# Fourier–Hyena encoder layer: within each sum, the products of the first parts placed ahead of those with a second part, and some casts and copies placed elsewhere

## The chip, the cores and the metric

The kernel runs on one core of one Trainium2 chip. TensorE (PE) multiplies matrices into PSUM, VectorE (DVE), ScalarE (ACT) and GpSimd (POOL) work elementwise, SyncE (SP) and POOL issue the transfers between HBM and SBUF. The metric is the device time of the one launch in microseconds, as a median over runs. Lower is better.

## The reference, cut to what matters

One encoder layer is applied to two sequences of 1024 rows and 1024 columns, called b=0 and b=1, in float32:

```
xn = rmsnorm(x, g_pre);  p = xn @ w_in                     # 1024 x 8192, split into
fv, fg, hv(3x), hg, mg(2x) = split(p)                      # 1024 columns each
y_f = (real(fft2 of fv by groups) * silu(fg)) @ w_fourier_out
v, x1, x2 = split(short_conv(hv))                          # width 3 along the rows
z = v
for n, gate in enumerate((x1, x2)):
    z = gate * long_conv(z, kf[:, n], d[n])                # by FFT of length 2048
y_h = (z * silu(hg)) @ w_hyena_out
g_f, g_h = split(sigmoid(mg + b_merge))
out = x + rmsnorm((g_f * y_f + g_h * y_h) @ w_out, g_post)
```

The filters kf come from a small network of sines and exponentials.

## The kernel before, in words

**Precision.** Almost all matrix products are made of rounded numbers. `split` (L168) turns a float32 tile into two parts that PE takes: the first part `h` is the rounded value, cast on ACT (L171), and the second part `l` is what is left, source minus `h`, a subtraction on DVE or POOL (L181). A product of a weight block w and a data block x is then three matmuls into one PSUM sum: h·h, h·l and l·h. `mm3` (L372) emits these three in a row, for one block of 128 rows of the contraction after the other. In the names below `wh`, `wl` are the two parts of a weight block, `xh`, `xl` those of the data, `bh`, `bl` and `yh`, `yl` those of the long convolution's data.

**Stages, in order of time.** (1) `phase_fourier`: normalisation, a copy of the normalised x to HBM (`d_x`), and the two-dimensional FFT as matrix products. (2) `phase_main`: first the 16 filter spectra (`pft`, `pXf`), with projections of b=0 between them as filling (`spill_gate`, PSUM tile `pin`, 128 by 1024, two banks); then `branches`, the long convolutions: 32 steps, 16 for each b. (3) `phase_gates`: the last projections of b=1 as 2 by 2 block products with fewer multiplications (`times`, PSUM `pg`). (4) `phase_out`: products with w_fourier_out (`pyf`) and w_hyena_out (`pyh`), 32 of each, and beside them the loading and splitting of w_out (`beside`, `blocks`, `sums`). (5) `last_rows`: the product with w_out (`po`, again `times`), the norm and the stores.

**A step of `branches`.** `conv_front` of the next step (transposes `tph`, the radix-4 `butterfly` on DVE, casts `bh`, subtractions `bl`) and `gates` of the next step (projection of x1 or x2) are traced ahead of `conv_back` of the step itself. `conv_back` runs four groups: `pX` (forward matmuls), a product with the spectrum on DVE, `yh` on ACT, `yl` on DVE, `pT` (inverse matmuls). In every second step with b=0, `gates` also multiplies x2 by silu(hg): for channels c below 6 the projection hg lies in HBM already, is loaded into a tile `sg` (tag `gt`, three buffers, shared with other tiles), passes through Silu on ACT (L937) and is multiplied into x2 on POOL.

**Weights.** `inproj` (L726) takes its blocks in two halves q of four blocks each: load `wr`, cast `wh` on ACT, `wl` on POOL (1472 matmuls of each of the three kinds use them). For b=1 the conv projections reload `wh`, `wl` from HBM. In the output stages `weight` (L1116) loads `wr` by POOL's queue, with `wh` on ACT and `wl` on DVE; three sets of buffers take turns.

**What sets the order.** The code is traced, and a scheduler of the tile framework, with a cost model of its own, orders the instructions of each engine ahead of the run. On the chip each engine and each queue takes its instructions in that fixed order, and waits by semaphores. `issue_after(i)` makes what is traced inside it stand behind instruction i on i's engine.

## Time and profile before

| | us |
|---|---|
| median of 3 runs (lowest, highest) | 2466.59 (2461.57, 2469.35) |
| the profiled execution, its own time | 2470.75 |
| its span, from the first to the last instruction | 2469.0 |
| PE busy in the span | 2407.5 (98%) |
| DVE busy | 1912.8 (77%) |
| ACT busy | 1064.4 (43%) |
| POOL busy | 499.0 (20%) |

PE's busy time is the union of matmuls whose modelled ends overlap, so a busy PE can still hold small gaps. An entry "A <- B" in a list of waits means that an instruction of A was idle until B released it; a line such as L194 is that of a helper through which all matmuls go, so groups are told apart by tiles. "PEclk" is the granted share of TensorE's clock.

### The profile page before, as it was taken

The numbers are of one execution on the slowest core, as the hardware profiler recorded it, in microseconds if no ns is written. First come the engines' busy times: TensorE is split into PE (matmuls) and PEld (weight loads), VectorE is DVE, ScalarE is ACT, GpSimd is POOL, SyncE is SP. The second block draws the span as 40 slices with busy tenths as digits, with TensorE's granted clock in tenths as the row PEclk, the third lists the DMA queues.
The fourth block names the chain that finished last, engine by engine and source line by source line (L and its number), as shares of the span: only waits on it lengthen the run. The fifth ranks groups of instructions, "written<-read, shape, count | busy, mean of one in ns | idle before, by whom it ended". The sixth has DMA issues, their size and how long they took to land.

```text
span 2469.0 us, 36969 instructions
## 1 busy us (share of the span) xinstructions
PE 2407.5 (98%) x13196; PEld 2086.9 (85%) x13196; DVE 1912.8 (77%) x3597; ACT 1064.4 (43%) x1919; POOL 499.0 (20%) x516
## 2 busy tenths in 40 slices
PE   6999999999999999999999999999999999999998
PEld 6988888888788888888888888888788788787786
DVE  7687898998649999899889999866556455665677
ACT  5546576766433333333222222323444344444343
POOL 1331213221342443331000000112100111112121
PEclk9999999999999999999999999999999999999999
DMA  7535655555555455545443443435444567775443
GB/s 274 183 122 205 217 182 166 169 180 168 171 174 179 159 176 163 172 149 203 137 134 131 143 142 131 133 128 176 161 162 158 193 218 255 237 268 194 156 160 128
DMA packets 225153, 429.37 MB, mean 174 GB/s; under 512 B 23542, under 2 KB 87255, under 8 KB 224456
## 3 DMA queue, kind: packets, MB, share of 16 engines
q1 hardware_dynamic: 198444, 333.34, 40.7%
q0 software_dynamic: 26336, 93.65, 10.7%
q8 instruction: 104, 1.70, 0.3%
q14 instruction: 81, 0.66, 0.1%
q10 hardware_dynamic: 188, 0.02, 0.0%
HBM read 290.60 MB, written 136.31 MB: 173 GB/s over the span
## 4 chain that ended last, share of the span: by engine, by line
PE 44%; DMA 4%; issue 4%; DVE 1%; POOL 1%; ACT 1%; SPq 0%; DVEq 0%; POOLq 0%; ACTq 0%
PE pin L194 17%; PE pg L194 8%; PE po L194 6%; PE pT L194 4%; PE pyf L194 4%; PE pX L194 4%; PE pyh L194 1%; DMA wr<-in_w_ho 1%; DMA wr<-in_w_fo 1%; POOL wr L1123 1%; PE tph L791 1%; DMA mraw<-d_m 1%; DMA d_m<-yf 1%; DMA t4l<-d_t 0%; DMA d_g<-gt 0%
## 5 line engine op out<-in xcount | busy, mean ns | idle before, releaser
L194 PE MATMUL pin<-xh,wl 128*128 128x512 f32 x1472 | 578.7, 393 | 3.3 <-POOL wl L181 3.3
L194 PE MATMUL pin<-xh,wh 128*128 128x512 f32 x1472 | 578.9, 393 | 1.1 <-DMA wh<-d_w 1.1
L194 PE MATMUL pin<-xl,wh 128*128 128x512 f32 x1472 | 577.5, 393 | 0.6 <-DVE xl L181 0.6
L181 POOL TENSOR_TENSOR wl<-wr,wh 128x512 fp32r<-128x512 f32 x136 | 246.2, 1811 | 1142.8 <-ACT wh L171 739.2
L194 PEld LDWEIGHTS pin<-xh,wl 128*128 128x128 f32 x1472 | 277.8, 189 | 54.9 <-POOL wl L181 4.1
L194 PEld LDWEIGHTS pin<-xl,wh 128*128 128x128 f32 x1472 | 277.7, 189 | 51.8 <-DVE xl L181 1.0
L194 PEld LDWEIGHTS pin<-xh,wh 128*128 128x128 f32 x1472 | 278.0, 189 | 51.3 <-DMA wh<-d_w 1.7
L171 ACT CAST wh<-wr 128x512 fp32r<-128x512 f32 x264 | 162.9, 620 | 326.1 <-PE pin L194 109.4
L194 PE MATMUL pT<-cinv,yh 128*128 128x256 f32 x1024 | 192.4, 283 | 4.4 <-ACT yh L171 4.4
L194 PEld LDWEIGHTS pT<-cinv,yh 128*128 128x128 f32 x1024 | 165.0, 191 | 13.9 <-ACT yh L171 4.9
L171 ACT CAST yh<-y 128x512 fp32r<-128x512 f32 x128 | 79.5, 621 | 202.5 <-DVE y L181 148.0
L181 DVE TENSOR_TENSOR t<-pX,k 128x1024 f32<-128x1024 f32 x128 | 155.5, 1215 | 14.2 <-PE pX L194 13.6
L194 PE MATMUL pyf<-sf,wh 128*128 128x512 f32 x512 | 159.1, 393 | 2.0 <-ACT wh L171 2.0
L194 PE MATMUL pX<-bh,cfwd 128*128 128x256 f32 x768 | 159.7, 286 | 0.0
L194 PE MATMUL pyh<-sh,wh 128*128 128x512 f32 x512 | 158.0, 390 | 1.6 <-ACT wh L171 1.6
L171 ACT CAST bh<-b 128x512 fp32r<-128x512 f32 x144 | 88.9, 619 | 135.1 <-DVE b L181 79.5
L181 DVE TENSOR_TENSOR wl<-wr,wh 128x512 fp32r<-128x512 f32 x128 | 87.4, 686 | 76.7 <-ACT wh L171 76.7
L194 PE MATMUL pT<-cinv,yl 128*128 128x256 f32 x512 | 145.3, 284 | 0.5 <-DVE yl L181 0.5
L194 PEld LDWEIGHTS pX<-bh,cfwd 128*128 128x128 f32 x768 | 125.8, 191 | 3.3
L194 PEld LDWEIGHTS pyf<-sf,wh 128*128 128x128 f32 x512 | 96.7, 189 | 22.8 <-ACT wh L171 2.8
L181 DVE TENSOR_TENSOR bl<-b,bh 128x512 fp32r<-128x512 f32 x144 | 102.6, 721 | 16.6 <-ACT bh L171 16.3
L194 PEld LDWEIGHTS pyh<-sh,wh 128*128 128x128 f32 x512 | 96.0, 188 | 22.2 <-ACT wh L171 2.5
(347 smaller groups left out, 5255.6 us busy)
## 6 DMA issues: line engine op xcount, KB each, us to landing
k<-d_k SPq DMA_DIRECT2D x128, 512.0 KB, 3.9
wr<-in_w_in SPq DMA_DIRECT2D x136, 256.0 KB, 3.1
d_g<-gt SPq DMA_DIRECT2D x124, 256.0 KB, 2.7
d_k<-kt SPq DMA_DIRECT2D x128, 128.0 KB, 2.2
d_k<-kt SPq DMA_DIRECT2D x64, 256.0 KB, 2.5
wr<-in_w_fo POOLq DMA_DIRECT2D x64, 256.0 KB, 3.3
g<-d_g SPq DMA_DIRECT2D x64, 256.0 KB, 3.7
wr<-in_w_ho POOLq DMA_DIRECT2D x64, 256.0 KB, 3.3
```

The costliest lines, as they stand in the source:

```text
L171: self.rounded = nc.scalar.copy(h, src)
L181: e.tensor_tensor(out, a, b, op=op)
L194: return self.nc.tensor.matmul(out, lhsT, rhs, start=start, stop=stop, skip_group_check=shared)
L791: nc.tensor.transpose(tp[:, q * P:(q + 1) * P], eo[:, e, q], self.ident)
L1123: nc.gpsimd.dma_start(r, a[w][dt][:, 512 * q:512 * q + 512])
```

## The change

It changes no operation and no size: on every engine the same instructions with the same shapes are there, apart from two fewer loads of an ACT table (21 for 23). What differs:

1. In `inproj`, `project`, `times`, `forward` and `conv_back`'s inverse products, all products of the first parts `wh` (or, in `forward` and `conv_back`, of the data's first part) come ahead of those with the weight's (the data's) second part.
2. `close(i + 1)`, behind `conv_back(i)`, now holds the Silu and the product with `sg` for the early channels, on ACT behind the step's last `yh` cast. Both loads of `sg` stay in `gates`.
3. In `phase_gates`, the last job's kept copy `v` goes into a buffer of the tag `f` of that stage, no longer into one of the two buffers `w` that the output stage's `wr` takes next.
4. In `phase_out`, `beside` also stands behind the last `wl` on DVE (`weighed2`), and the sums of w_out's blocks are traced two column blocks later (`part == 5`) than its splits. `sum4` only loads; its casts and subtractions (`t4h`, `t4l`) move to the first job of `last_rows`.
5. In `last_rows`, `prepare(i + 1)` stands on ACT behind the copy `u` of job i.

```diff
@@ forward
-            self.mm3(X[:, i], tab(pr, 0), (h[:, 0:2], l[:, 0:2]), True, False)
-            self.mm3(X[:, i], tab(pr, 1), (h[:, 2:4], l[:, 2:4]), False, True)
+            for d, parts in ((h, (0, 1)), (l, (0,))):
+                for k in range(2):
+                    for t in parts:
+                        self.mm(X[:, i], tab(pr, k)[t], d[:, 2 * k:2 * k + 2], d is h and k + t == 0, d is l and k == 1)
@@ inproj
-            for n in range(2):
-                for kk in range(4):
-                    k = 4 * q + kk
+            for w, xs in ((h, (self.xh, self.xl)), (l, (self.xh,))):
+                for n in range(2):
                     s = slice(512 * n, 512 * n + 512)
-                    self.mm3(ps[:, s], (h[:, kk], l[:, kk]), (self.xh[k][:, s], self.xl[k][:, s]), k == 0, k == 7)
+                    for kk in range(4):
+                        k = 4 * q + kk
+                        for x in xs:
+                            self.mm(ps[:, s], w[:, kk], x[k][:, s], w is h and x is self.xh and k == 0, w is l and k == 7)
@@ conv_back
-                    self.ended = self.mm3(out, w, R, i == 0, i == 1)
+                    todo += [(0, out, yh[:, i, r], R[0], i == 0, False), (0, out, yh[:, i, r], R[1], False, False),
+                             (1, out, yl[:, i, r], R[0], False, i == 1)]
+                for _, *m in sorted(todo, key=lambda m: m[0]):
+                    self.ended = self.mm(*m)
@@ branches, gates
                     if early:
-                        nc.sync.dma_start(sg, self.d_g[0][4][c][:, 512 * q:512 * q + 512])
-                    with tc.issue_after(self.turned.ins):
-                        nc.scalar.activation(sg, sg if early else ps[:, 512 * q:512 * q + 512], AF.Silu)
-                    self.mul("pool", x[:, 512 * q:512 * q + 512], x[:, 512 * q:512 * q + 512], sg)
+                        nc.sync.dma_start(sg[q], self.d_g[0][4][c][:, s])
+                    else:
+                        nc.scalar.activation(sg[q], ps[:, s], AF.Silu)
+                G[i] = sg, early
...
+        def close(i):
+            if i in G:
+                sg, early = G.pop(i)
+                for q in range(2):
+                    s = slice(512 * q, 512 * q + 512)
+                    if early:
+                        with tc.issue_after(self.rounded.ins):
+                            nc.scalar.activation(sg[q], sg[q], AF.Silu)
+                    self.mul("pool", X[i][:, s], X[i][:, s], sg[q])
...
             y = self.conv_back(n, c, B, ws)
+            close(i + 1)
@@ times
-        for k in range(4):
-            h, l = A[0][:, k], A[1][:, k]
-            for j, (w, x) in enumerate(((h, B[k][0]), (h, B[k][1]), (l, B[k][0]))):
-                m = self.mm(p, w, x, first and k + j == 0, k + j == 5, True)
+        todo = [(0, k, j) for k in range(4) for j in range(2)] + [(1, k, 0) for k in range(4)]
+        for w, k, j in todo:
+            m = self.mm(p, A[w][:, k], B[k][j], first and w + k + j == 0, w + k == 4, True)
@@ phase_gates
-                v = kept(pa)
+                v = kept(pa, last=i + 1 == len(jobs))
@@ phase_out
-                        self.mm3(ps, (h[:, kk], l[:, kk]), S[k], k == 0, k == 7)
+                        for x in S[4 * q + kk]:
+                            self.mm(ps, h[:, kk], x, 4 * q + kk == 0 and x is S[0][0], False)
+                    for kk in range(4):
+                        self.mm(ps, l[:, kk], S[4 * q + kk][0], False, 4 * q + kk == 7)
...
-                with tc.issue_after(self.fetched.ins), tc.issue_after(self.opened.ins):
+                with tc.issue_after(self.fetched.ins), tc.issue_after(self.opened.ins), tc.issue_after(self.weighed2.ins):
...
-                            blocks(k, self.raw)
+                            self.sum = blocks(k, self.raw)
+                        elif part == 5:
+                            sums(k, self.sum)
...
-                r = l.bitcast(F32)
-                nc.sync.dma_start(r, self.d_t[1][:, k])
-                self.split(h, l, r, "dve", "act")
+                nc.sync.dma_start(l.bitcast(F32), self.d_t[1][:, k])
@@ last_rows
             if i + 1 < len(jobs):
-                A = prepare(i + 1)
+                with tc.issue_after(fetched.ins):
+                    A = prepare(i + 1)
                 pa, pb, m1 = first(A)
+            if i == 0:
+                with tc.issue_after(kept_v.ins):
+                    for h, l in T4:
+                        self.split(h, l, l.bitcast(F32), "dve", "act")
```

The scheduler's result at three places. First, PE in a late projection of b=1 (`pin_18779`; `xh1_k` and `xl1_k` are the two parts of x's block k, `wh_18780` and `wl_18781` those of the weights of the first half). Its first six rows before:

```order
L194 MATMUL pin_18779<-xh1_0_13133,wh_18780 128x512
L194 MATMUL pin_18779<-xl1_0_13134,wh_18780 128x512
L194 MATMUL pin_18779<-xh1_0_13133,wl_18781 128x512
L194 MATMUL pin_18779<-xh1_1_13138,wh_18780 128x512
L194 MATMUL pin_18779<-xl1_1_13139,wh_18780 128x512
L194 MATMUL pin_18779<-xh1_1_13138,wl_18781 128x512
```

and with the change, from the 13th row of the same tile on:

```order
L194 MATMUL pin_18779<-xh1_2_13141,wh_18780 128x512
L194 MATMUL pin_18779<-xl1_2_13142,wh_18780 128x512
L194 MATMUL pin_18779<-xh1_3_13146,wh_18780 128x512
L194 MATMUL pin_18779<-xl1_3_13147,wh_18780 128x512
L194 MATMUL pin_18779<-xh1_0_13131,wl_18781 128x512
L194 MATMUL pin_18779<-xh1_1_13136,wl_18781 128x512
L194 MATMUL pin_18779<-xh1_2_13141,wl_18781 128x512
L194 MATMUL pin_18779<-xh1_3_13146,wl_18781 128x512
```

`wl` was the third matmul's operand; now 16 matmuls with `wh` stand ahead of the first with `wl`, and 8 with `wl` follow.

Second, ACT at the last early channel (c = 5) of `branches`, where `sg` is Silu's tile, `yh` the cast in `conv_back`, `bh` that of a butterfly. Before:

```order
L838 COPY T0s<-pT 128x512
L171 CAST wh<-wr 128x512
L171 CAST bh<-b_11100 128x512
L937 ACTIVATE sg<-sg 128x512
L171 CAST yh<-y 128x512
L171 CAST bh<-b_11101 128x512
L171 CAST wh<-wr 128x512
L758 ACTIVATE v<-pin,wsh 128x1024
```

and with the change:

```order
L845 COPY T0s<-pT 128x512
L171 CAST yh<-y 128x512
L171 CAST wh<-wr 128x512
L762 ACTIVATE x_12446<-pin,wsh 128x1024
L171 CAST bh<-b_12001 128x512
L171 CAST yh<-y 128x512
L957 ACTIVATE sg<-sg 128x512 x2
L845 COPY T1s<-pT 128x512
```

The second Silu of the channel stood in front of a `yh` cast that PE's next `pT` needs; both Silus now stand behind the last `yh` of a later `conv_back`.

Third, ACT at the first job of `last_rows` (`mraw` is the data of the next job, `u` and `m` are copies of PSUM tiles, `mxh` and `t4h` first parts). Before:

```order
L1286 COPY m<-po 128x512
L171 CAST wh<-mraw 128x512 x3
L1316 ACTIVATE sq,ss<-o 128x512
L1286 COPY u<-po 128x512
L171 CAST t4h_23691<-t4l_23692 128x512
L171 CAST mxh_23829<-ms_23825 128x512
```

and with the change:

```order
L1313 COPY m<-po 128x512
L1343 ACTIVATE sq,ss<-o 128x512
L1313 COPY u<-po 128x512
L171 CAST wh<-mraw 128x512 x2
L171 CAST mxh_23821<-ms_23817 128x512
L171 CAST mxh_23825<-ms_23816 128x1024
L1313 COPY m<-po 128x512
L171 CAST t4h_23418<-t4l_23419 128x512
```

The copy `u`, which frees PE's accumulator, no longer stands behind three casts of the next job's data. At the start of the output stage, ACT's casts of the first two weight halves of w_fourier_out now stand ahead of the eight casts of that stage's first data (`sf`), where they stood behind them.

More of the change, by code (lines that the diff above doesn't have):

```diff
@@ L173, in split @@
             nc.vector.tensor_copy(h, src)
-        self.sub(eng, l, src, h)
+        self.left = self.sub(eng, l, src, h)
     def stt(self, eng, out, a, s, b, op0=MUL, op1=ADD):
@@ L918, in branches @@
         plain = list(self.PLAIN)
-        Z, X = {}, {}
+        Z, X, G = {}, {}, {}
         def front(i):
@@ L1050, in out, with kept @@
                 nc.sync.dma_start(self.d_g[b][sec][c][:, s], t)
-            def kept(p, own=False):
-                t = gw.tile([P, 512], F32, tag="u", name="u", bufs=1) if own else wp.tile([P, 512], F32, tag="w", name="m", bufs=2)
+            def kept(p, own=False, last=False):
+                if own or last:
+                    t = gw.tile([P, 512], F32, tag="u" if own else "f", name="u" if own else "v", bufs=1 if own else 3)
+                else:
+                    t = wp.tile([P, 512], F32, tag="w", name="m", bufs=2)
                 copied = nc.scalar.copy(t, p)
@@ L1126, in weight @@
                 self.split(h.rearrange("p a b -> p (a b)"), l.rearrange("p a b -> p (a b)"), r, "dve", "act")
-                self.weighed = self.rounded
+                self.weighed, self.weighed2 = self.rounded, self.left
                 return h, l
@@ L1193, in blocks, with sums @@
                 self.sums(s, r)
+                return s
+            def sums(k, s):
                 h, l = [bl.tile([P, 2, 512], F32R, tag=f"{t}{k}", name=f"{t}{k}", bufs=1) for t in ("th", "tl")]
@@ L1285, in kept @@
             t = wp.tile([P, 512], F32, tag="gt" if own else "w", name="u" if own else "m", bufs=3 if own else 2)
-            nc.scalar.copy(t, p)
+            self.copied = nc.scalar.copy(t, p)
             return t
@@ L1332, in last_rows @@
             w = kept(pa, True)
+            fetched = self.copied
             pc = self.psum("T", 2, "po")
@@ L1337, in last_rows @@
             half_row(1, 1, pc, v, SUB, "pool")
-            last = (A, pa, pc)
+            last, kept_v = (A, pa, pc), self.copied
             if i + 1 < len(jobs):
-                A = prepare(i + 1)
+                with tc.issue_after(fetched.ins):
+                    A = prepare(i + 1)
                 pa, pb, m1 = first(A)
+            if i == 0:
+                with tc.issue_after(kept_v.ins):
+                    for h, l in T4:
+                        self.split(h, l, l.bitcast(F32), "dve", "act")
             A_, pa_, pc_ = last
```

14 lines of the change are left out of this document (7 added, 7 removed).

## The prediction, made before the changed kernel ran

> **What bounds the kernel now.** I read the stretches of time by stage first, then who made PE wait, then the timeline at each longer wait.
>
> By stage (us; then busy time of PE, PEld, DVE, ACT, POOL with instructions; granted clock, DMA share, GB/s):
>
> ```profile
> 0.00:262.00 262.00, 230.08 (x1680) 214.78 (x1681) 193.78 (x466) 147.36 (x292) 68.38 (x94) 0.99 0.57 194
> 712.00:1172.00 460.00, 453.99 (x2683) 401.55 (x2682) 428.98 (x698) 159.69 (x251) 154.76 (x146) 0.99 0.51 170
> 1172.00:1630.00 458.00, 458.00 (x2740) 407.55 (x2739) 407.17 (x722) 130.14 (x206) 14.91 (x8) 1.00 0.40 135
> 1941.00:2300.00 359.00, 352.74 (x1534) 287.71 (x1533) 205.82 (x315) 162.97 (x269) 68.67 (x128) 1.00 0.68 231
> 2300.00:2469.00 169.00, 157.00 (x685) 129.18 (x683) 123.15 (x255) 65.31 (x134) 31.41 (x29) 0.97 0.44 147
> ```
>
> PE is the bound in every stage. Of its 61.5 us without work, 32 lie in the Fourier stage, whose instruction order the change leaves as it is until its tail, and 12 in the last stage, all but 2 of them behind its last matmul. What an edit of order can win lies in the short waits in between. Two rows of the chain of waits (start, us) give what PE takes when nothing is late: 4.11 us for 18 matmuls of 512 columns is 0.228 each, 2.87 for 24 of 256 columns 0.12 each.
>
> ```profile
> 1126.47 4.11 PE pin L194 x18
> 1123.59 2.87 PE pT L194 x24
> ```
>
> PE's waits from 640 us on (total us, times, longest), all of them:
>
> ```profile
> PE pT L194 <- ACT yh L171: 4.4, 1, 4.4
> PE pin L194 <- POOL wl L181: 3.3, 2, 2.4
> PE po L194 <- ACT u L1286: 2.0, 1, 2.0
> PE pyf L194 <- ACT wh L171: 2.0, 2, 1.6
> PE pyh L194 <- DVE wl L181: 1.8, 2, 1.3
> PE pyh L194 <- ACT wh L171: 1.6, 2, 1.5
> PE pin L194 <- DMA wh<-d_w: 1.1, 1, 1.1
> PE pg L194 <- DVE wl L181: 0.8, 1, 0.8
> PE pT L194 <- DVE yl L181: 0.5, 1, 0.5
> PE pyf L194 <- DVE wl L181: 0.5, 1, 0.5
> ```
>
> They sum to 18.0 us in 14 waits. Two things come on top. A matmul's drawn length is about 0.39 us while the next could start after 0.228, so each wait hides 0.16 more: 2.2 in all. And the clock falls after four of them:
>
> ```profile
> 653.50:656.90 3.40, 2.91 (x10) 2.63 (x11) 0.00 (x0) 0.00 (x0) 1.67 (x2) 0.50 0.51 141
> 988.00:994.80 6.80, 4.83 (x12) 3.90 (x13) 4.68 (x6) 3.81 (x6) 4.06 (x6) 0.50 0.68 242
> 1957.40:1960.80 3.40, 3.40 (x9) 2.65 (x8) 0.69 (x1) 0.04 (x1) 0.99 (x2) 0.50 0.65 223
> 2315.80:2319.20 3.40, 3.40 (x9) 2.64 (x10) 3.37 (x5) 1.12 (x2) 0.71 (x1) 0.50 0.23 74
> ```
>
> PE worked 2.91 + 4.83 + 3.40 + 3.40 = 14.54 us at clock 0.50, half of which, 7.3 us, is lost. So the ceiling of what the change can win is 18.0 + 2.2 + 7.3 = 27.5 us.
>
> [...]
>
> **The change part by part.** No instruction is added, so every term is a wait taken away.
>
> *Silu of the early channels.* In the 4.4 us wait, ACT sat 7.13 us in front of a Silu whose tile was still to land, with `yh` queued behind it:
>
> ```profile
> 978.54 8.84 POOL L181 TENSOR_TENSOR x<-x,sg 128x512 f32<-128x512 f32 x2 [6.58 <-ACT wh L171]
> 988.78 0.63 ACT L937 ACTIVATE sg<-sg 128x512 f32<-128x512 f32 x1 [7.13 <-DMA sg<-d_g]
> 989.97 0.79 PE L194 MATMUL pT<-cinv,yh 128*128 128x256 f32 x2 [4.45 <-ACT yh L171]
> ```
>
> Two products on POOL took 8.84 us and held the buffer that the load needed. With the change the Silus stand behind the step's last `yh`, and both loads are issued a step earlier (32 steps fill the 918 us from 712 to 1630, some 28 us each). I take the whole wait and its clock: 4.4 + 0.16 + 4.83/2 = 7.0 us.
>
> *`wl` after 16 matmuls in the projections.* `wl` on POOL normally takes 1.29 us; at 646 us two took 8.96, and PE stood:
>
> ```profile
> 639.50 1.29 POOL L181 TENSOR_TENSOR wl<-wr,wh 128x512 fp32r<-128x512 f32 x1 [5.67 <-ACT wh L171]
> 646.21 8.96 POOL L181 TENSOR_TENSOR wl<-wr,wh 128x512 fp32r<-128x512 f32 x2 [5.42 <-ACT wh L171]
> 653.99 0.79 PE L194 MATMUL pin<-xh,wl 128*128 128x512 f32 x1 [2.44 <-POOL wl L181]
> ```
>
> 14 more matmuls ahead of it are 14 × 0.228 = 3.2 us of cover, more than the longest wait of 2.4: 3.3 + 0.3 + 2.91/2 = 5.1 us. `wh` is also given back after 16 matmuls of 24 where it was needed to the 23rd, 1.6 us sooner. The 1.1 us on its load at the turn to b=1 may have another cause, so I take half: 0.6. For `yl` the cover grows by two narrow matmuls, 0.24, half of its wait: 0.3. In `pg` it is 6 × 0.228 = 1.4 us against 0.8: 1.0 with the hidden part.
>
> *The output stage's `wl`* gets the same 1.4 us against a longest wait of 1.3. That alone would be narrow. At 2102 us the wait has a second cause, DVE's work for w_out just ahead of two `wl`:
>
> ```profile
> 2098.86 1.22 DVE L181 TENSOR_TENSOR bl<-oraw,bh 128x1024 fp32r<-128x1024 f32 x1
> 2100.59 1.22 DVE L181 TENSOR_TENSOR tl<-osum,th 128x1024 fp32r<-128x1024 f32 x1
> 2101.73 1.28 DVE L181 TENSOR_TENSOR wl<-wr,wh 128x512 fp32r<-128x512 f32 x2
> ```
>
> The `tl` goes two column blocks later. I take all: 1.8 + 0.5 + 3 × 0.16 = 2.8.
>
> *The output stage's `wh`.* At 1956 us `wh` stood behind a sigmoid waiting for its load; at 2281 behind a `t4h` doing so:
>
> ```profile
> 1954.98 0.72 ACT L1153 ACTIVATE g<-g,bm 128x512 f32<-128x512 f32 x1 [2.88 <-DMA g<-d_g]
> 1955.61 0.60 ACT L171 CAST wh<-wr 128x512 fp32r<-128x512 f32 x1
> 2281.03 0.62 ACT L171 CAST t4h<-t4l 128x512 fp32r<-128x512 f32 x1 [5.52 <-DMA t4l<-d_t]
> ```
>
> For the first, the freed buffer lets the loads run ahead and one more weight half is cast before that sigmoid; it feeds 12 matmuls, 2.7 us, against 1.6: 2.0 + 0.3 + 1.7 = 4.0. For the second, `t4h` is gone from there: 1.6 + 0.3 = 1.9. What `t4h` costs in its new place: four casts of 0.62 and four subtractions, needed only after 36 matmuls (8.2 us) behind the copy they follow. The DVE's sums for job 2 stand between, and their data was loaded with that of job 1. I cost it at nothing; without that cover it is up to 4 × 0.62 = 2.5 us.
>
> *The copy `u` in the last rows* stood behind casts that waited 6.72 us for data of the next job:
>
> ```profile
> 2312.83 1.66 ACT L171 CAST wh<-mraw 128x512 fp32r<-128x512 f32 x3 [6.72 <-DMA mraw<-d_m]
> 2315.02 0.56 ACT L1286 COPY u<-po 128x512 f32<-128x512 f32 x1
> ```
>
> Now it stands ahead of them. Those casts are needed 24 matmuls later, 5.5 us: 2.0 + 0.16 + 1.7 = 3.9.
>
> Sum: 7.0 + 5.1 + 0.6 + 0.3 + 1.0 + 2.8 + 4.0 + 1.9 + 3.9 = 26.6 us.
>
> **What comes back.** Almost every row of PE's order is new, and the scheduler's costs know neither an 8.84 us pair on POOL nor a late load. The old order left 18.0 us of waits in this way; the bounds for new ones are 0 and the whole 27.5. Waits for a second part (3.3 + 1.8 + 0.8 + 0.5 + 0.5 = 6.9) now meet more cover everywhere; the other 11.1, for casts, copies and loads, are cured at named places only and may open elsewhere. I take 8, nearer to 11.1 than to nothing. Net: 18.6 us.
>
> The profiled execution took 2470.75, of which 18.6 less is 2452; it stood 4.2 above the median of 2466.59, so the median goes to **2448 us**.
>
> **The rivals.**
>
> *DVE becomes the bound in the branches of b=0.* From 712 to 1172 us it is busy for 428.98 of 460. For: no other stage is as tight. Against: even with the stage 7.9 us shorter (7.0 + 0.6 + 0.3) it has 23 us free. Then these 7.9 are not won: 2456.
>
> *New waits take the place of the old* all over, since an order by wrong costs is as blind as before. For: 18.0 us were left by it. Against: the added cover of 1.4 to 3.2 us, above most waits in the list. Net 0 to 7: 2463.
>
> *POOL starves at the moved products (slower).* The six pairs x·`sg` now stand together behind the end of `conv_back`, where DVE combines its groups without a pause, and the next `wl` is queued behind them. Minimum, median and maximum in ns:
>
> ```profile
> L181 POOL TENSOR_TENSOR x<-x,sg x16: 1257/1302/7621, 754.0 to 1145.4; 128x512 f32<-128x512 f32 x16
> L181 POOL TENSOR_TENSOR wl<-wr,wh x46: 1252/1489/4414, 710.9 to 1128.6; 128x512 fp32r<-128x512 f32 x46
> ```
>
> From the last `yh` to that `wl` the new order has at least 32 matmuls of 512 columns, 68 of 256 and 8 narrower on PE: 7.3 + 8.2 + 0.9 = 16.3 us. With every product at its maximum the way is 0.6 (`yh`) + 1.3 (two Silus) + 15.2 + 0.6 (an issue) + 4.4 = 22.1: 5.8 us late, six times 35, against 26.6 won: with the clock falling each time, about 2480. It decides from products of 4.7 us each on; the median is 1.3.
>
> [...]
>
> **How the numbers follow.** Forecast 0.76; DVE 0.10; new waits 0.10; POOL 0.04. The range, 2439 to 2463, goes from the ceiling (2466.6 − 27.5) to the second rival. 0.3% (7.4 us), about what three runs can tell from no change, puts the bounds at 2459.2 and 2474. The forecast lies below the first, as does most of the DVE case; most of the second rival lies between: faster 0.82, same 0.13, slower 0.05.
>
> **What would show it.** In the list of PE's waits after: no `pT` behind ACT's `yh` of several us, no `pin` behind POOL, no `po` behind `u`; a clock of 0.50 only in the Fourier stage; the stages 640 to 1172, 1941 to 2300 and 2300 to the end shorter by about 12, 8 and 4 us less what came back. Wrong would be: a new wait of over 2 us, above all one behind POOL's x·`sg`, or `pc`'s last sum behind `t4h` in the first job of the last rows; DVE over 98% from 712 on with PE waiting for it; or the waits gone and the time not, which would say that the matmuls themselves became slower in the new order.

## The result and the profile after

| | before | after |
|---|---|---|
| median, us (lowest, highest) | 2466.59 (2461.57, 2469.35) | 2448.88 (2445.80, 2449.50) |
| ratio of the two, with its 95% interval | | 0.9923 (0.9909 to 0.9938) |
| the profiled execution, its own time | 2470.75 | 2449.50 |
| its span | 2469.0 | 2447.4 |

The changed kernel is faster by 0.77%, some 18 us. In its profile the longest waits of PE are other ones than before, and far fewer are left. These are the head of the page and the list of PE's waits from 640 us on (us in total, times, longest) of the changed kernel:

```profile
span 2447.4 us, 36994 instructions
PE 2397.8 (98%) x13196; PEld 2083.9 (85%) x13196; DVE 1933.1 (79%) x3597; ACT 1059.9 (43%) x1917; POOL 497.3 (20%) x516
...
PE pyf L194 <- ACT wh L171: 2.8, 3, 1.5
PE pX L194 <- DVE bl L181: 1.8, 2, 1.0
PE pyh L194 <- ACT wh L171: 0.5, 1, 0.5
PE pX L194 <- DVE t L181: 0.4, 1, 0.4
```

None of the ten entries of before is as it was: nothing waits for POOL, for `yh`, for `u` or for any `wl`. Two stand in both lists, `pyf` and `pyh` behind ACT's `wh`, but at other places. The 18.0 us have become 5.5. The stages (columns as in the view by stage of before):

```profile
0.00:262.00 262.00, 228.02 (x1665) 213.13 (x1666) 193.51 (x464) 145.88 (x290) 66.19 (x94) 0.98 0.56 193
...
712.00:1172.00 460.00, 457.85 (x2726) 405.55 (x2725) 445.38 (x708) 164.52 (x258) 151.22 (x143) 1.00 0.51 170
1172.00:1630.00 458.00, 458.00 (x2728) 406.93 (x2727) 410.13 (x719) 128.24 (x204) 12.26 (x9) 1.00 0.41 136
1929.00:2285.00 356.00, 352.67 (x1549) 290.05 (x1549) 206.16 (x316) 161.46 (x268) 67.57 (x126) 1.00 0.69 232
2285.00:2447.40 162.40, 152.29 (x672) 125.79 (x670) 119.96 (x253) 64.94 (x134) 31.43 (x28) 0.98 0.45 149
```

Between the Fourier stage and the last matmul (at 2437 us) no stretch at clock 0.50 is left, where the kernel before had four; the 0.98 of the last row comes from behind the last matmul.

**Lost time, the measure used below.** The list of waits leaves out short stalls and does not tell what a lower clock costs. So, for each pair of neighbouring matmuls, I took the time from start to start, less the median of that time for the first one's shape, and added these up by stage. I call it PE's lost time. In the fourteen profiles that follow, the span less all lost time lies between 2390.3 and 2390.9 us. So the time of every kernel here is one constant plus what PE loses: the median matmul of each shape became no slower in the new order. In us, by stage (Fourier to 262 us; filter spectra to the first `pX`; branches to the last `pin`; gates to the first `pyf`; output to the first `po`; last rows):

| kernel | span | Fourier | spectra | branches | gates | output | last rows | sum behind Fourier |
|---|---|---|---|---|---|---|---|---|
| before | 2469.0 | 39.9 | 8.6 | 14.1 | 0.9 | 11.2 | 3.7 | 38.6 |
| after | 2447.4 | 42.9 | 2.3 | 7.2 | −0.3 | 4.6 | −0.2 | 13.6 |
| e1, all orders, no moves | 2447.2 | 40.7 | 2.3 | 7.0 | −0.3 | 2.2 | 4.4 | 15.6 |
| e2, all moves, old order | 2447.6 | 39.5 | 6.6 | 7.8 | 1.1 | 2.3 | −0.2 | 17.6 |
| e3, after without the Silu's move | 2436.8 | 38.0 | 2.3 | 5.1 | −0.1 | 0.9 | −0.2 | 8.0 |
| e4, after with the last rows of before | 2442.8 | 39.6 | 2.3 | 7.4 | −0.2 | 1.6 | 1.3 | 12.4 |
| f1, order of pX and pT alone | 2461.6 | 39.0 | 4.3 | 9.1 | −0.3 | 14.1 | 4.7 | 32.0 |
| f2, order of inproj alone | 2458.2 | 37.4 | 5.1 | 8.2 | 1.4 | 13.7 | 1.7 | 30.1 |
| f4, order of pg, po, pyf, pyh alone | 2458.7 | 38.2 | 8.1 | 17.0 | −0.3 | 3.5 | 1.5 | 29.8 |
| e6, the Silu's move alone | 2460.7 | 39.1 | 8.8 | 7.5 | −0.1 | 12.9 | 1.9 | 31.0 |
| n3, gates traced first | 2461.5 | 38.6 | 8.1 | 11.7 | 1.7 | 9.3 | 1.9 | 32.6 |
| e7, e3 with a fourth buffer for g | 2437.9 | 39.6 | 2.3 | 6.1 | 0.0 | −0.5 | −0.2 | 7.7 |
| e8, e7 with the order in the Fourier stage | 2436.9 | 39.3 | 2.3 | 5.8 | −0.2 | −0.5 | −0.2 | 7.2 |
| e10, e7 with the old order in inproj | 2440.6 | 37.9 | 4.0 | 9.1 | −0.3 | −0.5 | −0.2 | 12.1 |

Each row is one execution. The Fourier column goes from 37.4 to 42.9, although up to 215 us only e8 changes the order of its matmuls. In f4 every matmul up to 1752 us stands in the order of before, and its branches lose 17.0 us for 14.1. So a difference of three us between two profiles, in any stage, may be nothing but that.

### The profile page after: what moved, and what is told of

Same layout as the page of the kernel before. It is cut to its first block, busy times and chain, and to the rows that moved or that the text cites. A ratio compares the mean times of both kernels' runs of the same rounds, so it can differ in the third digit from the quotient of the medians.

```text
span 2447.4 us, 36994 instructions
## 1 busy us (share of the span) xinstructions
PE 2397.8 (98%) x13196; PEld 2083.9 (85%) x13196; DVE 1933.1 (79%) x3597; ACT 1059.9 (43%) x1917; POOL 497.3 (20%) x516
## 4 chain that ended last, share of the span: by engine, by line
PE 46%; issue 4%; DMA 3%; DVE 2%; POOL 1%; ACT 1%; SPq 0%; DVEq 0%; POOLq 0%; ACTq 0%
PE pin L194 18%; PE pg L194 7%; PE po L194 6%; PE pT L194 5%; PE pX L194 4%; PE pyh L194 3%; PE pyf L194 2%; DMA g<-d_g 1%; DMA wr<-in_w_fo 1%; PE tph L795 1%; POOL wr L1145 1%; DMA wr<-in_w_ho 1%; DMA t1l<-d_t 0%; DMA oraw<-in_w_out 0%; DVE t L181 0%
## 5 line engine op out<-in xcount | busy, mean ns | idle before, releaser
L194 PE MATMUL pin<-xh,wl 128*128 128x512 f32 x1472 | 385.7, 392 | 0.0
L194 PEld LDWEIGHTS pin<-xh,wl 128*128 128x128 f32 x1472 | 270.3, 188 | 50.6
L194 PE MATMUL pT<-cinv,yh 128*128 128x256 f32 x1024 | 164.0, 282 | 0.0
L194 PEld LDWEIGHTS pT<-cinv,yh 128*128 128x128 f32 x1024 | 146.1, 190 | 7.1
L194 PE MATMUL pX<-bh,cfwd 128*128 128x256 f32 x768 | 133.2, 286 | 0.4 <-DVE t L181 0.4
L194 PE MATMUL pyf<-sf,wh 128*128 128x512 f32 x512 | 126.9, 390 | 2.8 <-ACT wh L171 2.8
L194 PE MATMUL pyh<-sh,wh 128*128 128x512 f32 x512 | 126.6, 389 | 0.5 <-ACT wh L171 0.5
L194 PEld LDWEIGHTS pX<-bh,cfwd 128*128 128x128 f32 x768 | 111.5, 190 | 4.9 <-issue 0.9
L194 PE MATMUL pT<-cinv,yl 128*128 128x256 f32 x512 | 104.1, 285 | 0.0
```

Of the source, the lines that this page charges most:

```text
L194: return self.nc.tensor.matmul(out, lhsT, rhs, start=start, stop=stop, skip_group_check=shared)
```

## The experiments

Two theories were set against each other at first. **Named waits**: every wait has a cause of its own, and the part of the change that takes the cause away wins it. **The cover**: the order of the matmuls does nearly all, since a late second part costs nothing once its matmuls stand last. A third, **luck**, stood in the first expectations as a rival only, and came to the fore when the first four runs together fitted neither: which wait stands where is an accident of one particular order, and any new order loses the old accidents and draws others.

### The two halves of the change

e1 is the kernel before with all five orders and none of the moves:

```diff
@@ kernel before: forward, inproj, conv_back, times, phase_out
-   h h, h l, l h for each block of the contraction
+   all products with a first part of weights (or data), then those with the second
    close(), weighed2, the buffer v, part == 5, T4 and fetched.ins: as before
```

> The kernel before, with the five changes of matmul order alone: in each sum the products of the first parts ahead of those with a second part. The Silus, the buffer of v, the sums of w_out, t4h and the last rows' casts stay as they were. Theory (each part takes away its own waits): the waits for a second part go, 5.1 + 1.0 + 2.8 + 0.6 + 0.3 = 9.8 us, so about 2457; PE still waits for ACT's yh (about 4 us) or for u in the last rows (about 2 us), each with a stretch of clock 0.50 behind it. Rival (the cover does it all, the moves do nothing): 2449, and those waits are gone too. Second rival (any new order by the same scheduler has other waits, none belongs to a part): anywhere from 2445 to 2467, with waits in other places than the list of before.

Measured: 2445.84 us (2440.66 to 2448.94), ratio 0.9909 (0.9895 to 0.9923). The order alone wins 22 us of a median of 2467.92 in that session. Named waits had allowed 10 of them. The list of PE's waits of e1, its three longest:

```profile
PE po L194 <- ACT u L1294: 2.6, 1, 2.6
PE pyf L194 <- ACT wh L171: 1.6, 1, 1.6
PE pin L194 <- DMA wh<-d_w: 0.6, 1, 0.6
```

The wait for `u`, which a move cures, is still there, as it should be. But the wait of 4.4 us for `yh` is gone without the Silu's move, and the waits for `wh` in the output stage have shrunk from 3.6 to 1.6 without the freed buffer and without `t4h`'s move.

e2 is the other half, the change with its order undone:

```diff
@@ changed kernel: forward, inproj, conv_back, times, phase_out
-   all products with the first part, then those with the second
+   h h, h l, l h for each block of the contraction
```

> The changed kernel with the three products of each sum in the old order (h h, h l, l h block by block), and all the moves kept. Theory: the moves win 7.0 + 4.0 + 1.9 + 3.9 = 16.8 us, so about 2450; in PE's list waits for a wl (on POOL in the projections, on DVE in the output stage) stand again, some 5 us in all, and none for yh behind a Silu or for u. Rival (the cover does it all): 2465, with waits for first parts as well. With both halves alone, the sum of the two gains against the 17.7 us of the whole tells whether they add up: the theory has 9.8 + 16.8 less what comes back twice.

Measured: 2451.53 us (2449.01 to 2453.32), ratio 0.9934 (0.9922 to 0.9946), where named waits had said 2450. The waits for a `wl` that stand again sum to 3.4 us (2.2 on POOL in the projections, 0.9 in `pg`, 0.3 in the output stage), where some 5 had been expected. So the halves win 22 and 16 us by themselves, and 18 together. They are not additive: both of them end the same waits, above all that for `yh` and those in the output stage. These two rows are all that e2, with the old order, still waits for in the output stage:

```profile
PE pyf L194 <- ACT wh L171: 0.3, 1, 0.3
PE pyh L194 <- DVE wl L181: 0.3, 1, 0.3
```

And beside the orders the moves win nothing that can be told: e1's ratio (0.9895 to 0.9923) and that of the whole change (0.9909 to 0.9938) overlap, and e1's median is the lower one.

### Parts of the moves

e3 takes the Silu's move alone out of the change:

```diff
@@ changed kernel, branches, gates
-   nc.sync.dma_start(sg[q], ...)        # Silu and product with sg in close(i + 1)
+   nc.sync.dma_start(sg, ...)
+   with tc.issue_after(self.turned.ins):
+       nc.scalar.activation(sg, sg if early else ps[...], AF.Silu)
+   self.mul("pool", x[...], x[...], sg)
@@ branches
-   close(i + 1)
```

> The changed kernel with the Silu of the early channels and the product with sg back in gates, as before; all else as changed. Theory: the wait of pT for yh behind the Silu returns, up to 4.4 us with its clock, so +7.0: about 2456. Rival: the wait was one accident (one of six channels had it) that another order does not repeat: 2449, the Silus still ahead of some yh casts, and ACT's waits for the load of sg covered.

(In the changed kernel `close` holds the products with `sg` of all eight channels of b=0, and the Silus of the six early ones; e3 puts back both.)

Measured: 2440.99 us (2438.67 to 2448.03), ratio 0.9899 (0.9885 to 0.9914). The named waits had forecast 7 us more than the changed kernel takes; by the medians it is 8 us less, with intervals that just overlap. Its profiled execution is the shortest of its five, that of the changed kernel the longest of its five. Its list of PE's waits, complete from 640 us on, and ACT's wait for `sg` in the branches:

```profile
PE pyf L194 <- ACT wh L171: 0.8, 1, 0.8
PE pin L194 <- DMA wh<-d_w: 0.7, 1, 0.7
PE pX L194 <- DVE t L181: 0.4, 1, 0.4
```

```profile
ACT sg L944 <- DMA sg<-d_g: 12.2, 7, 4.8
```

ACT still stands in front of a Silu for up to 4.8 us (12.2 in seven times; 19.1 in seven before), and PE feels nothing of it. So the Silu in front of `yh` was not enough to make the wait. In the kernel before a pair of POOL products of 8.84 us held the buffer as well; the longest single product of e3 took 2.28 us.

e4 takes the moves at the last rows out of the change:

```diff
@@ changed kernel, phase_out and last_rows
-   nc.sync.dma_start(l.bitcast(F32), self.d_t[1][:, k])     # split in last_rows
+   nc.sync.dma_start(r, self.d_t[1][:, k]); self.split(h, l, r, "dve", "act")
-   with tc.issue_after(fetched.ins):
-       A = prepare(i + 1)
+   A = prepare(i + 1)
```

> The changed kernel with the casts and subtractions of t4 back in the output stage, and with the next job's casts in the last rows no longer behind the copy u; all else as changed. Theory: the copy u waits behind casts for data still loading again, 2.0 us and 1.7 of clock, and the wait for wh behind t4h in the output stage, 1.9: +5.8, about 2454.7. Rival: the first parts' order gives the sums enough cover here as well: 2449 to 2451.

Measured: 2448.76 us (2444.59 to 2452.20), ratio 0.9926 (0.9913 to 0.9939), as the changed kernel. Its trace does have the wait back:

```profile
PE po L194 <- ACT u L1315: 1.2, 1, 1.2
```

and its last rows lose 1.3 us where the changed kernel loses nothing. That is the sign that was expected, with 1.5 us for 3.9. The other wait that was expected, of `pyh` for `wh` behind `t4h`, is not in its list, and the output stage gained more than was lost (4.6 to 1.6) by an order that nobody aimed at.

### Luck against cause

n3 is the kernel before with two lines swapped, and holds neither cover nor cure:

```diff
@@ kernel before, branches
-   nxt = front(i + 1)
-   gates(i + 1)
+   gates(i + 1)
+   nxt = front(i + 1)
```

> The kernel before, with one swap in the branches: the gates of the next step are traced ahead of its conv_front instead of behind it. No matmul inside a sum changes its place, no copy or cast is moved to cure a wait, so there is neither cover nor cure in it. Theory of the named waits (each wait has its own cause, and only an edit that takes the cause away wins it): about 2467, within 3 us, as before. Theory of the cover (a second part that is late costs nothing once its matmuls stand behind): also about 2467. The rival, luck (a product on POOL becomes long where it happens to fall under a run of VectorE's instructions, and any new order deals these anew; the kernel before had drawn one of 7.6 us in front of the only wait of 4.4 us): the 4.4 us wait and its half clock go, others may come, and the time moves by several us either way, most likely to 2455 to 2463.

Measured: 2464.69 us (2454.69 to 2469.23), ratio 0.9989 (0.9978 to 1.0000). Some of its list:

```profile
PE pin L194 <- POOL wl L181: 3.5, 2, 2.1
PE pyf L194 <- ACT wh L171: 2.3, 1, 2.3
PE po L194 <- ACT u L1286: 1.8, 1, 1.8
PE pg L194 <- DVE wl L181: 1.7, 1, 1.7
...
PE pin L194 <- DVE xl L181: 1.2, 1, 1.2
```

The 4.4 us for `yh` are gone, with nothing done about them; the waits whose causes were named (`pin` behind POOL, `pyf` behind `wh`, `u`) are all still there; and new ones have come (`pg` 1.7 for 0.8, `xl` 1.2). So the one wait went as the theory of luck has it, most of the others stayed as the named waits have it, and the time is nearly that of before.

e6 makes the Silu's move alone:

```diff
@@ kernel before, branches
+   close(i + 1)     # early Silus behind the step's last yh, and both products with sg
```

> The kernel before, with the second part of the change alone: the early channels' Silu and the product with sg stand behind the step's last yh. Theory of the named waits: the term for Silu, 7.0, so about 2460. Theory of the cover: nothing is covered; at most the 4.4 us wait goes, 2460 too. Luck: the first wait goes, as it would with any other order, and the POOL products, moved together, fall under VectorE's runs elsewhere: anything from 2455 to 2470, with waits of PE's projections on POOL's wl that sum to over 3 us.

Measured: 2463.99 us (2458.10 to 2467.07), ratio 0.9987 (0.9977 to 0.9997). The wait for `yh` is gone and the branches lose 7.5 us for 14.1, which is 6.6 of the 7.0 that were named; by the medians of the runs 2 us are left of it. In this profile the output stage loses 1.7 more than before.

The long product of before comes in several orders, and it does not need the Silu's place. These rows are of POOL's products with `sg` in n3, in f2 (below) and in the changed kernel, with minimum, median and maximum in ns:

```profile
L181 POOL TENSOR_TENSOR x<-x,sg x16: 1284/1520/5835, 747.7 to 1138.6; 128x512 f32<-128x512 f32 x16
```

```profile
L181 POOL TENSOR_TENSOR x<-x,sg x16: 1287/1455/7720, 747.5 to 1136.2; 128x512 f32<-128x512 f32 x16
```

```profile
L181 POOL TENSOR_TENSOR x<-x,sg x16: 1270/1332/2050, 784.2 to 1137.4; 128x512 f32<-128x512 f32 x16
```

f2 has one of 7.72 us, longer than the 7.62 of before, and its `yh` waits 1.4 us at the most, at another place. So a long product by itself did not make the wait either.

### The orders one by one

f2 has the new order in `inproj` alone, f1 in `forward` and `conv_back` alone, f4 in `times` and the two output products alone:

```diff
@@ f2: kernel before, inproj
-   self.mm3(ps[:, s], (h[:, kk], l[:, kk]), (self.xh[k][:, s], self.xl[k][:, s]), k == 0, k == 7)
+   for w, xs in ((h, (self.xh, self.xl)), (l, (self.xh,))): ...
@@ f1: kernel before, forward and conv_back
-   self.mm3(X[:, i], tab(pr, 0), (h[:, 0:2], l[:, 0:2]), True, False) ...
+   for d, parts in ((h, (0, 1)), (l, (0,))): ...
@@ f4: kernel before, times and phase_out
-   self.mm3(ps, (h[:, kk], l[:, kk]), S[k], k == 0, k == 7) ...
+   products with h of all four blocks, then those with l
```

> The kernel before, with the new order in inproj alone: 16 matmuls with wh ahead of the 8 with wl. Forward, inverse products, block products and output stages keep h h, h l, l h, and nothing is moved. Theory of the named waits: it wins the terms for wl in pin (5.1) and the load of wh (0.6), so about 2461. Theory of the cover: the projections hold the only second parts that POOL makes, with runs of up to 7.7 us, so most of the 22 us of the run with all five orders comes from here: about 2450. Luck: the wait of 4.4 us goes too although nothing is done about it, 5.1 + 0.6 + 7.0, about 2454, and new waits can take some of it back.

> The kernel before, with the new order in the long convolutions alone (pX and pT). Theory of the named waits: it wins 0.3 us (the wait for yl), so about 2466, and the wait of 4.4 us stays. Theory of the additive orders: what the run with all five won, 22, less inproj's 4 and the output stages' part, so several us from here too. Luck: the wait of 4.4 us goes, as it did with the gates traced first and with inproj's order alone, both without a cure for it, and other waits come in its place: 2458 to 2465.

> The kernel before, with the new order in the block products and the output stages alone (pg, po, pyf, pyh): all products with wh of a half ahead of those with wl. Projections and long convolutions keep the old order, and nothing is moved. Theory of the named waits: it wins the terms for pg (1.0) and for the output stage's wl (2.8), and leaves the waits for wh and for the copy u: 3.8, so about 2462; in the list of waits no pyh, pyf or pg behind wl, but pyf behind ACT's wh (about 2), pyh behind ACT's wh (about 1.5) and po behind u (about 2). Theory of the additive orders (the orders are worth what the run with all five won, 22, less the 4 of inproj's): some 12 to 18 us from here, about 2451. Luck: the waits of the stages ahead change too although nothing there is moved; 2455 to 2467.

| | median, us | ratio | won, us | named waits had said |
|---|---|---|---|---|
| f2 | 2462.02 (2455.54 to 2467.77) | 0.9978 (0.9966 to 0.9990) | 5.4 | 5.7 |
| f1 | 2459.11 (2454.98 to 2463.39) | 0.9965 (0.9951 to 0.9979) | 8.6 | 0.3 |
| f4 | 2457.66 (2455.76 to 2461.48) | 0.9962 (0.9950 to 0.9975) | 9.3 | 3.8 |

(Won is 1 − ratio, times the median of before in these sessions, 2466 to 2468.) The three together are 23.3, and e1, which has all three, won 22.4. That looks as if the orders added up, but the table by stage says that the agreement is in part luck: against the kernel before, the output stage loses 2.3 us less in f1, f2 and f4 taken together and 9.0 less in e1, and the last rows 3.2 less together and 0.7 more in e1. The theory of additive orders had also put f4 at 12 to 18 us. Only the order of `inproj` is worth what was named. The other two are worth more, and the stages tell where. In f4 the output stage goes from 11.2 to 3.5, though nothing was moved there. The first two waits of its list, those of its output stage and last rows, and the row of ACT where `t4h` waits for its load just as before:

```profile
PE pT L194 <- ACT yh L171: 4.6, 1, 4.6
PE pin L194 <- POOL wl L181: 4.0, 2, 2.1
PE pyf L194 <- ACT wh L171: 2.1, 4, 0.8
PE po L194 <- ACT u L1287: 1.4, 1, 1.4
...
PE pyh L194 <- ACT wh L171: 0.3, 1, 0.3
```

```profile
2284.96 0.62 ACT L171 CAST t4h<-t4l 128x512 fp32r<-128x512 f32 x1 [7.56 <-DMA t4l<-d_t]
```

ACT stands there for 7.56 us, longer than the 5.52 of before, and PE waits 0.3 for it where it waited 1.5. One explanation is that buffers come free sooner: with the old order a half's `wh` is needed until its 11th matmul of 12, now until its 8th, so ACT may cast the next one three matmuls or 0.7 us sooner, each time. ACT's own waits go with it, but do not show it: `wh` waited 124.2 us for PE to give a buffer back in the output stage before (72.0 behind `pyf`, 52.2 behind `pyh`) and 106.1 in f4 (48.5 and 57.6), yet 107.6 (47.1 and 60.5) in e2 too, which keeps the old order. So what shortened the waits for `wh` in f4 stays open. Those that remain are short: the longest of f4's in that stage is 0.8 us.

In f1 the wait of 4.4 us is gone (`yh` is not in its list), and so is the one for POOL at 646 us, whose stage takes the new order of `forward` too; two others, for POOL's `wl` at 1713 and 1731 us, stand in the list for 2.2 in all. That is luck for the first, as in n3. For the second I cannot say which it is.

The first line of f4's list tells what kind of luck that is. Ahead of 1752 us f4 has the very order of the kernel before, and it repeats the whole pattern: a pair of POOL products of 8.85 us, ACT 7.25 us in front of the Silu, PE 4.6 us in front of `pT`. So the wait is no accident of one execution; it belongs to the order, comes back as long as the order stays, and goes when the order is another.

The waits for a second part behave differently, over all fourteen kernels. Each of the seven with the old order in `inproj` (before, e2, e6, f1, f4, n3, e10) has one or two waits of `pin` for POOL's `wl`, in the lists from 640 us on; none of the seven with the new order has any. Each of the six with the old order in the output products waits for `wl` there, and none of the eight with the new one. As f2 differs from before and e10 from e7 in the order of `inproj` alone, the cover is a cause there, whatever else an order does.

### From the experiments to a faster kernel

What the changed kernel and e3 still lose in the output stage lies in ACT's queue: a sigmoid waits for its load, and `wh` is queued behind it. ACT's rows of the changed kernel at the longest wait (1.49 us at 2213.95):

```profile
2212.67 0.72 ACT L1177 ACTIVATE g<-g,bm 128x512 f32<-128x512 f32 x1 [5.33 <-DMA g<-d_g]
2213.30 1.12 ACT L171 CAST wh<-wr 128x512 fp32r<-128x512 f32 x2
```

This is the pattern of 1956 us before. e7 is e3, with a fourth buffer for these tiles:

```diff
@@ e3, phase_out
-   g = wp.tile([P, 512], F32, tag="gt", name="g", bufs=3)
+   self.ng = getattr(self, "ng", -1) + 1
+   g = (sp.tile([P, 512], F32, tag="g", name="g", bufs=1) if self.ng % 4 == 3 else
+        wp.tile([P, 512], F32, tag="gt", name="g", bufs=3))
```

> The changed kernel without its second part (as the run with the Silu put back, 2441.0), and in the output stage every fourth tile g of a sigmoid in a buffer of its own: four buffers in place of three, so that a sigmoid need not wait for a load that waits for a buffer. Theory of the named waits: ACT's waits for g, which hold up the cast of wh behind them, fall from about 45 us to under 25, and the waits of pyf for ACT's wh go (0.8 us in the run with the Silu put back, 2.8 us in the changed kernel, 1.1 and 1.5 of it in one piece): about 2440. Luck: the output stage is ordered anew and waits come elsewhere in it; 2438 to 2445.

Measured: 2439.34 us (2437.84 to 2439.66), ratio 0.9886 (0.9873 to 0.9899). The changed kernel's row of ACT's waits for `g` has no counterpart in e7's list, where 2.6 us of waiting for such a load are left, in front of a load of ACT's table at the sigmoid's line. That row of the changed kernel:

```profile
ACT g L1177 <- DMA g<-d_g: 45.3, 16, 5.3
```

These are all waits of e7's PE from 640 us on:

```profile
PE pin L194 <- DMA wh<-d_w: 1.1, 1, 1.1
PE pX L194 <- DVE t L181: 0.4, 1, 0.4
PE tph L795 <- ACT xt L796: 0.2, 1, 0.2
PE pT L194 <- ACT yh L171: 0.2, 1, 0.2
```

So the loads were late for want of a buffer (21.4 us of ACT's time before, 35.6 in e3, both with three buffers), and that is a cause, not luck: e8 and e10, which have the fourth buffer in other orders, have no such row either. What it is worth in time is not settled, since the intervals of e7 and e3 overlap.

e10 asks what `inproj`'s cover is worth in that cleaner kernel:

```diff
@@ e7, inproj
-   for w, xs in ((h, (self.xh, self.xl)), (l, (self.xh,))): ...
+   self.mm3(ps[:, s], (h[:, kk], l[:, kk]), (self.xh[k][:, s], self.xl[k][:, s]), k == 0, k == 7)
```

> The fastest version so far (the changed kernel with the Silu put back and a fourth buffer for g, 2439.3), with inproj's order put back to h h, h l, l h. Theory of the named waits: the wait for POOL's wl at the end of the filter spectra comes back, 2.1 to 2.4 us with its half clock, 2443 to 2445; on it the rest of the order has no influence, since it lies ahead of all the other edits. Theory that the cover is worth more among other edits than alone (not additive): 2450 or more, with waits in the branches. Luck: up to 2443 without that wait.

Measured: 2442.77 us (2441.49 to 2443.33), ratio 0.9898 (0.9883 to 0.9913). By the medians that is 3.4 us more than e7 and 3.8 more than e8 of the same session (the intervals overlap). That is about the amount that named waits had said, but not by their mechanism: the wait at 650 us did not come back, as only the theory of luck had allowed (up to 2443 without it). PE waits 2.7 us for POOL's `wl` at 1711 and 1729 us instead. The expectation had overlooked that `forward`'s new order, which this kernel keeps, lies in the stage around 650 us too.

e8 puts the new order into the Fourier stage too:

```diff
@@ e7, stage() of the Fourier transforms (pse, pso)
-   for m in range(4):
-       self.mm3(pe if m < 2 else po, data(m), (seq[:, 0, e, m], seq[:, 1, e, m]), ...)
+   for o, ms in ((pe, (0, 1)), (po, (2, 3))):
+       products of data(m)[0] for both m, then those of data(m)[1]
```

> The fastest version so far (2439.3) with the new order in the Fourier stage's products over the rows as well (pse, pso): the products of the data's first part ahead of those with the second, which leaves 4 matmuls of 256 columns ahead of the first second part, not 2. Theory of the named waits: of the 39.6 us that this stage loses, some 7 lie ahead of pse and pso, and only those behind a second part can go: 1 to 3 us, about 2437. Theory that this stage waits for its loads: nothing, 2439.3 within 1. Rival: the whole order after it changes with it and new waits come, 2440 to 2445.

Measured: 2438.97 us (2438.57 to 2442.14), ratio 0.9886 (0.9873 to 0.9900): the same as e7. That stage's 39 us do not hang on its second parts. e7 and e8 have the lowest medians here and lie below the changed kernel (their intervals end at 0.9899 and 0.9900, its own begins at 0.9909); from e3 they cannot be told apart.

## Why the prediction was right, and where not

The time was right: 2448 for 2448.88. That the edits would end most of the waits was right as well. But the working gave wins to the wrong parts, and two errors cancelled; that the figure came within one us is luck.

**The ceiling** of 27.5 us was somewhat too low. Behind the Fourier stage 38.6 us were lost, and e3, which is a part of the change, loses 8.0, which is 30.6 less: short stalls that stand in no list of waits can be won too.

**The sum.** The terms sum to 26.6; the stages behind the Fourier stage lost 25.0 less (38.6 − 13.6). By stage: spectra and branches 13.2, where the terms make 13.0; gates 1.2 (1.0); output 6.6 (8.7); last rows 3.9 (3.9).

**The Silu, 7.0.** The size is there in the trace (e6, branches 14.1 to 7.5). The step that failed is "I take the whole wait" as something that this part wins: n3 and f1 lose the wait without it, e1 too, and the change without it (e3) is not slower but probably faster: 2440.99 for 2448.88, though the intervals just overlap. The wait was an accident of one order, and I had its ingredients in front of me: a product of 7621 ns where the median is 1302.

What the moved products do cost was looked for on the wrong side. The rival had POOL starving behind DVE. POOL didn't: its longest product with `sg` took 2050 ns, and PE waits for no `wl`. It was DVE's instructions that took longer, beside POOL's. These are the changed kernel's rows of POOL and then of DVE, PE's wait behind them last:

```profile
1069.11 2.58 POOL L181 TENSOR_TENSOR x<-x,sg 128x512 f32<-128x512 f32 x2 [5.24 <-ACT sg L957]
1071.65 1.33 POOL L181 TENSOR_TENSOR wl<-wr,wh 128x512 fp32r<-128x512 f32 x1
...
1069.49 2.35 DVE L177 SCALAR_TENSOR_TENSOR b<-b,xt 128x128 f32<-128x128 f32 x2
1071.76 1.37 DVE L177 SCALAR_TENSOR_TENSOR b<-bs,xt 128x128 f32<-128x128 f32 x1
1073.06 0.48 DVE L177 SCALAR_TENSOR_TENSOR b<-b,xt 128x128 f32<-128x128 f32 x2
...
1074.40 0.50 PE L194 MATMUL pX<-bl,cfwd 128*128 128x256 f32 x2 [1.03 <-DVE bl L181]
```

Two instructions that take 0.48 us together took 2.35 beside the two products, and a third of 0.28 took 1.37 beside the `wl`: 3.0 us more than they need, ahead of the `bl` that PE then waits for. The other half of that entry, 0.75 us at 816.59, has no such pair ahead of it.

**`wl` in the projections, 5.1 and 0.6.** Right: f2 won 5.4, e10 lost about 3.4 by the way back, and no kernel with the new order in `inproj` has a matmul that waits for POOL behind 640 us. One thing was missed: `forward`'s order serves the filter spectra as well, and f1 had lost the wait at 646 us without `inproj`'s.

**`yl` 0.3, `pg` 1.0, the output's `wl` 2.8.** Right, as far as the lists tell: all of these waits are gone with the orders alone (e1; gates 0.9 to −0.3). The second cause that I named for the output's `wl`, DVE's `tl`, fits what e2 shows, which has only the moves: 0.3 us of that wait are left.

**The output's `wh`, 4.0 and 1.9.** The waits named did go, but the step that gave them to the moves alone failed. The moves do end them without the orders (e2 loses 2.3 us in that stage); the orders end most of them without the moves too (f4 has neither the freed buffer nor `t4h`'s new place and wins 7.7 of that stage's 11.2). I had counted that `wh` is given back sooner in `inproj`, and not in the output stages; whether that is f4's reason is not shown. The step also left out that `g` has three buffers: in the changed kernel the same pattern stands at three other places, which cost PE 1.1, 0.5 and 1.5 us.

**The copy `u`, 3.9, and T4 at nothing.** Right: the last rows lose −0.2 for 3.7, no wait stands behind `t4h`, and the wait for `u` is in every kernel without this move and in none with it. On the chip it did not stand out: e4 and the changed kernel have the same median.

**What comes back, 8.** Too high for the stages that I meant: 25.0 of 26.6 stayed won. The waits of the changed kernel sum to 5.5, but the order also ended short stalls that no term held, and none of the new waits costs clock. Against that, its profiled execution lost 3.0 us more in the Fourier stage (42.9 for 39.9). From one profile to the other that makes 2470.75 − 25.0 + 3.0 = 2448.8, with the 2449.50 of the changed kernel's profile 0.7 above. I had taken 2452 for the profiled execution and then 4.2 off for the median; the median of the changed kernel lies only 0.6 below its profile. So the estimate of 8 was too high by about 6, and the Fourier stage (3.0) and the place of the two profiles within their runs (3.6) took that back: luck, not working.

**The rivals.** DVE was busy for 445.38 of 460 us in the branches of b=0, and PE for 457.85: it did not become the bound. New waits did not take the place of the old ones in this kernel. They nearly did in n3, which shows that the case was a real one. In the POOL rival PE's matmuls add up to 16.4 us, not 16.3, which changes nothing.

**The half clock.** Before, the waits of 4.4, 2.4, 2.0 and 1.6 us were followed by 0.50, others of 1.5 and 1.3 us were not. The length alone does not decide it: the wait of 2.2 us in e2 was followed by 1.00. What went with the clock, in the profiles of before and after, was how much of one window of 3.41 us was idle, as the last section shows.

## What to carry to other kernels

A row that shows a wait also shows one order's accident: before a wait is counted as won by the edit that names it, look for an ingredient that is far from its median, and make a control that changes the order and cures nothing; a part whose gain the control also gets is not worth its code. What lasted over every order tried here is what gives slack everywhere: the late operand's matmuls placed last, and one buffer more. And take the edits out one by one afterwards: here one of them probably cost more than it won.

## What the runs showed of the hardware

**Stretches at clock 0.50 began in steps of 3.41 us.** In the trace's clock record of the kernel before, the seven starts of stretches at 0.50 lie whole multiples of 3.41333 us apart, to within 2 ns, and so do the three of the changed kernel; those ahead of the last matmul lasted 3.41 or 6.83 us. Take these steps as windows, from 240 us on and ahead of the last matmul. Of the windows that ran at full clock themselves, four were idle for 2.12 to 2.65 us in sum (counted as lost time is, each loss put just ahead of the matmul that came late), all of them before, and each was followed by a window at 0.50. The next longest, 1.77 us at 2211.77 in the changed kernel and 1.61 at 2100.76 before, were followed by 1.00, and so were all shorter ones; between 1.77 and 2.12 us these two profiles have none. So in them the clock went not with a wait's length alone, but with how much of one window it filled. The same wait, for POOL's `wl` at 650 us, in the kernel before and in e2 (the columns of the view by stage; the clock is the third figure from the end):

```profile
650.09:653.50 3.41, 1.46 (x7) 0.88 (x5) 2.72 (x10) 2.67 (x5) 3.41 (x1) 1.00 0.00 0
653.50:656.92 3.42, 2.93 (x10) 2.65 (x11) 0.00 (x0) 0.00 (x0) 1.67 (x2) 0.50 0.51 141
```

```profile
648.70:652.10 3.40, 2.10 (x10) 1.40 (x8) 3.09 (x12) 2.73 (x5) 3.40 (x1) 1.00 0.00 0
652.10:655.50 3.40, 2.53 (x16) 2.26 (x17) 0.00 (x0) 0.63 (x2) 2.05 (x2) 1.00 0.43 132
655.50:658.90 3.40, 3.40 (x22) 3.01 (x21) 2.09 (x6) 2.17 (x6) 0.00 (x0) 1.00 0.74 258
```

Before, 2.44 us of waiting left PE busy for 1.46 us of one window, and the next ran at 0.50; in e2, at its 2.2 us, PE was busy for 2.10 and 2.53 us of two such stretches, and both are followed by 1.00. The spread of the runs goes with the clock: of the 29 executions of the kernel before that stand beside n3, the shortest (2459.92) had a mean clock of 0.996 and the longest (2472.32) 0.993. The waits of one profile do not tell the spread, though: e7, with only one wait over half a us, spreads over 2 us in four executions, and e3, whose longest wait is 0.8 us, over 9 in five (clock 0.998 to 0.996).

**POOL's and DVE's instructions took longer beside each other, both ways.** In the profile of the kernel before, POOL has 152 `wl` and products with `sg`, each with two SBUF operands of 128x512. The 36 that had DVE instructions with two SBUF inputs beside them for less than 5% of their time took 1.25 to 1.30 us. The two longest took 7.73 us (the `wl` at 646.21, within the 8.96 us pair that the prediction shows) and 7.62 us (the product at 978.54), each beside an unbroken run of such DVE instructions (20 and 18 of them). They ended 1.12 and 1.14 us behind the last of that run, about the 1.3 us that the 36 took. Such DVE instructions fill 79% of the time of the 21 over 2.5 us (with overlaps counted once), and 33% of that of the 86 under 1.4 us. The other way round, in the changed kernel, a DVE instruction that takes 0.28 us in the median took 1.37 beside one POOL subtraction of 1.33. So the two long POOL instructions lasted to the end of the run beside them and about one usual length more; why, no trace here shows.

**What stays open.** Why the output stage of e3 loses 0.9 us and that of the changed kernel 4.6, when they differ in the branches alone, was not settled; the loads of `g` are late in both (35.6 and 45.3 us of ACT's time). No run took the freed buffer of `v`, or the later sums of w_out, out by itself. Each comparison by stage rests on one execution of each kernel. The 39 us of the Fourier stage were not studied beyond e8.
